# Placing the block merges of the first heads seven steps later in a hybrid conformer and delta-rule trunk

## The chip, the cores and the metric

The kernel runs on one core of a Trainium2 chip. The time is that of one execution on the device, in microseconds, and lower is better. The kernel before takes 2454.08 us (median of three runs, 2453.21 to 2454.3).

The engines are named as in the profile: PE is TensorE (the matmuls), PEld its weight loads, DVE is VectorE, ACT is ScalarE, POOL is GpSimd, SP is SyncE, whose queue here issues every DMA. Each engine has one queue of instructions and works through it in order; an instruction that waits holds back everything behind it on that engine.

## The reference

Two layers act on an input of 1024 tokens by 1024 features, all in float32. The first mixes tokens with a conformer convolution, the second with a gated delta rule; each is followed by a squared-relu layer of 4096 hidden features, and a norm ends the work.

```python
for i in range(DEPTH):                       # DEPTH = 2
    hn = rms_norm(h, norm_mix_g[i])
    mix = conformer_conv(...) if i == 0 else gated_deltanet(...)
    h = h + mix
    h = h + sqrelu_mlp(rms_norm(h, norm_ffn_g[i]), mlp_w1[i], mlp_w2[i])
return rms_norm(h, final_norm_g)
```

The change lies in the gated delta rule. It has 8 heads of 128 features for keys and for values. Each head goes through the tokens in chunks and has, in each chunk, to solve a triangular system with ones on the diagonal:

```python
kk = jnp.einsum('bhnid,bhnjd->bhnij', k_beta, k) * decay
m = jnp.where(strict, kk, 0.0) + jnp.eye(CHUNK, dtype=jnp.float32)
sol = lax.linalg.triangular_solve(m, rhs, left_side=True, lower=True, unit_diagonal=True)
```

After that a scan over the chunks carries a 128 x 128 state for each head.

## The kernel before, in words

**Halves and products.** The tokens are worked in two halves of 512. All large layers are chains of *products*: one product is 128 output features by 512 tokens, over 1024 input features. To keep float32 accuracy on float32r matmuls, weights and activations are split in a high and a low part, so a product is 8 x 3 = 24 matmuls (L178 to L180): high weights by high and by low activations, low weights by high activations. For each product SP loads 512 KB of weights (L130), ACT makes the high part wh (L138) and DVE the low part wl (L139). There are two buffers each for the raw weights, wh and wl, and three PSUM tiles for the results.

**Steps.** The delta rule goes on beside the products. It is written as Python generators; `tick` advances each running generator by one `yield`. A tick is traced after matmul 15 of each product (L182) and after what follows each product, so a step is half a product.

**Lanes.** In each half `gdn_in` makes the projections of head after head, four products for each, and `gdn` runs the delta rule for pairs of heads in two lanes: lane 0 takes heads 0, 1 and then 4, 5; lane 1, started 40 steps behind, takes heads 2, 3 and then 6, 7. After the projections come the products of a squared-relu layer of the other half.

**One head pair, `delta`.** In order: keys and queries are loaded and transposed, and their norms taken. For each head: gr, the sums of the decays, is loaded (L693), ACT and DVE make the decays e, POOL multiplies them by the two triangular masks (el L706, e L708); PE makes g1 = k k^T (L714) and DVE turns it into X with el (L717), whose 32 x 32 diagonal blocks go to DRAM (L722); PE makes g2 (L728), DVE makes AT from it with e (L731). Then one pair at a time, kept apart by the list `inverting`: the blocks come back as fx (L742), ft is cleared (L743, L744), and POOL inverts them by substitution (fm L749, ft L751, 31 times each, three to a step). The inverses go through DRAM (td L760) into the tile T (L763), and v is transposed and scaled (v1, L767). Here stands the loop of `INV` empty steps (L770). What follows it are the *merges*, which join the 32 x 32 inverses to the inverse U of a whole 128 x 128 chunk: ub, a transpose of T (L773), a memset of U on POOL (L779) and eight copies into U on DVE (L782); then four rounds of small matmuls, y1 to y4 (L789, L798, L818, L825), with copies between them, a step each. Then comes the scan (L831 to L866) and the gated norm.

**What sets the order.** The body only traces instructions. A planner then puts them into the engines' queues: it simulates the program with a cost for each instruction and gives an engine, among the instructions that are ready by its own clock, the one traced first (weights count as traced 300 instructions earlier, L193). It thus may move an instruction ahead of its step where nothing holds it, and an instruction traced later comes behind those traced earlier where all are ready. The order so found is fixed; on the chip each engine follows it, whatever the real durations are.

**Tiles.** Most tiles of the delta rule and of the projections' outputs come from pool g with 27 buffers; small results in PSUM come from pool pg with 5; fx, ft, T, ub, y1s, t6s and y3s have one buffer each.

Of the kernel before, what the change touches and what calls it, by code (L numbers as in the profile page):

```python
# [11 lines left out]
PSUM = bass.MemoryType.PSUM  # L12
DRAM = bass.MemoryType.DRAM

P = 128
D = 1024
S = 1024
KC = D // P            # feature chunks
HT = S // 2            # tokens of a half
NCH = HT // P          # chunks of the delta rule in a half  # L20
H = 8                  # heads
NQ = 4                 # parts of the hidden layer
# [3 lines left out]
HG = 2                 # heads that go through the delta rule together  # L26
# how each tile of the depthwise convolution is done, by half (v: the vector engine, a: ScalarE
# and Pool, p: Pool, s: the vector engine but for the last SHARED taps), and how many taps go
# between two steps
# [3 lines left out]
INV = 5                # steps from the inverses to what uses them  # L33
IJ = 3                 # steps of the substitution traced at a time
LANE = 40              # steps by which the second stream of heads is behind
AHEAD = 2              # products whose weights are under way
PRIO = 300             # by how much weights go before what was traced earlier
HB = 10                # tiles in the pools
AB = 17
GB = 27  # L40
NB = 6                 # conv tiles of the second half before the first half's layer norm
# norms whose sum of squares goes to TensorE as two float32r parts
# [9 lines left out]
def _body(ctx, tc, a, out):  # L52
# [25 lines left out]
    # [t, j] = 1 where t <= j, and its strict transpose  # L78
# [19 lines left out]
    def split(dst, src):  # L98
        """src as the sum of two float32r parts"""
        nc.scalar.activation(out=dst[:, 0, :], in_=src, func=AF.Copy)  # L100
        nc.vector.tensor_tensor(out=dst[:, 1, :], in0=src, in1=dst[:, 0, :].bitcast(F32),  # L101
                                op=ALU.subtract)
# [7 lines left out]
    # weights that stay for a second pass over them  # L110
    keep = [f"m2_11_{NQ - 1}{o}" for o in range(KC)]

    def weights(src, name, n=KC * P):
        """weights as the sum of two float32r parts"""
        if n < KC * P:
            # few columns: both parts side by side
            raw = wp.tile([P, KC * P], F32, tag="raw", name=f"raw_{name}")
            nc.sync.dma_start(raw[:, :n], src)
            r3 = raw[:, :n].rearrange("p (k m) -> p k m", k=KC)
            both = wp.tile([P, KC * P], F32R, tag="wh", name=f"wh_{name}")  # L120
            b4 = both.rearrange("p (k i m) -> p k i m", k=KC, i=2)
            nc.scalar.activation(out=b4[:, :, 0], in_=r3, func=AF.Copy)
            nc.vector.tensor_tensor(out=b4[:, :, 1], in0=r3, in1=b4[:, :, 0].bitcast(F32),
                                    op=ALU.subtract)
            return both, None
        raw = wp.tile([P, KC * P], F32, tag="raw", name=f"raw_{name}")
        # the first ones in parts, so that the products start early
        n = KC * P // (2 if name in ("pa0_0", "pb0_0") else 1)
        for c in range(0, KC * P, n):
            nc.sync.dma_start(raw[:, c:c + n], src[:, c:c + n])  # L130
        kept = name in keep
        wh = wp.tile([P, KC * P], F32R, tag="kh" if kept else "wh", name=f"wh_{name}",
                     bufs=KC if kept else 2)
        wl = wp.tile([P, KC * P], F32R, tag="kl" if kept else "wl", name=f"wl_{name}",
                     bufs=KC if kept else 2)
        for c in range(0, KC * P, n):
            s = slice(c, c + n)
            nc.scalar.activation(out=wh[:, s], in_=raw[:, s], func=AF.Copy)  # L138
            nc.vector.tensor_tensor(out=wl[:, s], in0=raw[:, s], in1=wh[:, s].bitcast(F32),  # L139
                                    op=ALU.subtract)  # L140
        return wh, wl

    # work that goes on beside the products: it is traced in steps between them
# [41 lines left out]
    # the products in their order; weights are fetched and split one product ahead  # L185
# [38 lines left out]
    def add_stats(ps, x, first=True, last=True):  # L224
        """means over the features, with the tokens on the partitions, a chunk to a column"""
        for t in range(NCH):
            nc.tensor.matmul(ps[:, t:t + 1], x[:, t * P:(t + 1) * P], mean_w[:, 0:1],
                             start=first and t == 0, stop=last and t == NCH - 1)

    def rstd_of_tokens(ps, name):  # L230
        """1 / sqrt(mean + eps) from such means, for all partitions with the tokens along them"""
        rs = sp.tile([P, NCH], F32, tag="rs", name=f"rs_{name}", bufs=2)
        nc.scalar.activation(out=rs, in_=ps[:, :NCH], func=AF.Sqrt, bias=eps[:, 0:1], scale=1.0)
        nc.vector.reciprocal(rs, rs)
        r = g_tile(f"rstd_{name}")[:, :HT]
        r3 = r.rearrange("p (c t) -> p c t", c=NCH)
        nc.vector.tensor_copy(r3, rs.unsqueeze(2).to_broadcast([P, NCH, P]))
        pt = pg.tile([P, NCH, P], F32, tag="pg", name=f"rt_{name}")
        for t in range(NCH):
            nc.tensor.transpose(pt[:, t, :], r3[:, t, :], ident)  # L240
        nc.scalar.activation(out=r3, in_=pt, func=AF.Copy)
        return r
# [15 lines left out]
    def norm(get, g, name, act, eng=nc.vector):  # L258
        """rms_norm of the half, split for the products, into act"""
# [13 lines left out]
    def norm_later(get, g, name, act):  # L273
        """rms_norm of the half but for 1 / rms, split into act; that factor is made meanwhile"""
# [88 lines left out]
    def own_taps(hf, ct):  # L363
        """how many taps of the tile are the vector engine's"""
        return {"v": CW, "s": CW - SHARED}.get(CONV[hf][ct][0], 0)
# [17 lines left out]
    def conv_pool(hf):  # L383
        """the taps that Pool adds up, by itself or from ScalarE's products"""
# [25 lines left out]
    def conv_vec(hf):  # L410
        """the vector engine's taps; the sum so far is in PSUM"""
# [27 lines left out]
    def layer_norm(hf, act):  # L439
# [8 lines left out]
        for k in range(KC):  # L448
            nc.vector.tensor_tensor(out=c[k], in0=c[k], in1=mu, op=ALU.subtract)
            sq = squares(c[k], f"ln{hf}{k}")  # L450
            # sums of two, or of all in the second half where TensorE has other work
# [57 lines left out]
    def mlp_out_last(l, hf, hid, q):  # L509
        """the end of the work: by quarters of the tokens, so that little is left after the last"""  # L510
# [38 lines left out]
    def ab(hf, act):  # L549
        """decays and betas of the half, tokens on partitions"""  # L550
        ps = dense(act, f"ab{hf}", 64)
        # rows 64.. have the share of the weights' low parts
# [15 lines left out]
        # what 1 + e rounded away  # L568
# [26 lines left out]
        # the sums of the decays with tokens along the row, for each head, in DRAM  # L595
# [8 lines left out]
    def gin(hf, act, h):  # L604
        """projections of a head, the short convolution, silu; to DRAM"""
# [38 lines left out]
    def delta(hf, h0, yo):  # L644
        """the delta rule for heads h0.. of the half; gated and normalised output into yo"""
# [44 lines left out]
        for i, h in enumerate(hh):  # L690
            # sums of the decays, the same on all partitions
# [47 lines left out]
        # inverses of the 32 x 32 diagonal blocks of 1 + X, a block to a partition  # L739
# [30 lines left out]
        for i in range(INV):  # L770
            yield
# [3 lines left out]
        # U is the transpose of the whole inverse: block by block  # L775
# [32 lines left out]
        # the inverse of the upper left quarter, not transposed  # L808
# [21 lines left out]
        # the scan  # L830
# [36 lines left out]
        # o is short of the factor rq / sqrt(dk); rec holds its square  # L867
# [42 lines left out]
    def final(hf, cols=slice(0, HT)):  # L910
# [18 lines left out]
        for k in range(KC):  # L929
            y = g_tile(f"fo{nm}{k}")[:, :n]  # L930
            if cols.start and k % 3 == 1:
                # the last ones are shared with Pool
# [21 lines left out]
    def gdn(hf, ready, yo, lane):  # L954
        """every other group of heads, once it has its inputs"""
        for h0 in range(lane * HG, H, 2 * HG):
            while h0 not in ready:
                yield
            yield from delta(hf, h0, yo)
# [83 lines left out]
def order(a):  # L1043
    """the products' names and weights, in their order"""
# [33 lines left out]
def arrange(i):  # L1078
    import numpy as np

    def cols(x):
        """[n * 128] -> [128, n]"""
        return np.asarray(x).reshape(-1, P).T
# [6 lines left out]
    def tiles(w):  # L1090
        """[K, N] -> [K / 1024 * N / 128, 128, 1024]: weights of 128 columns and 1024 rows"""
# [54 lines left out]
```

## Time and profile before

| what | value |
|---|---|
| times, three runs | 2453.21, 2454.08, 2454.3 us |
| profiled execution, span | 2454.3 us |
| PE busy | 2333.6 us, 95% |
| DVE busy | 1529.1 us, 62% |
| ACT busy | 1082.7 us, 44% |
| POOL busy | 973.5 us, 40% |
| granted PE clock, mean | 0.980 |
| DMA | 275.38 MB, mean 112 GB/s |

The span is the time from the first to the last instruction of the profiled execution. It equals the highest of the three times and is 0.2 us above the median. "Idle before" is the time an engine stood ahead of an instruction, and the releaser behind the arrow is the instruction whose end let it go. Matmuls overlap each other, so the durations in a row of PE are longer than the distance between two starts.

### The profile page before, as it was taken

Reading aid. Unit: us, or ns where it says so; the run is one execution under the profiler, and the core shown is the slowest. Engines: PE = TensorE matmul, PEld = TensorE weight load, DVE = VectorE, ACT = ScalarE, POOL = GpSimd, SP = SyncE. Lnnn points to the kernel's source line nnn. Section 1 sums busy time; section 2 is a strip of 40 time slices with the busy share of each in tenths; the row PEclk is TensorE's granted clock in tenths of the full one; section 3 lists DMA queues with packets and bytes.
Section 4 is the critical chain, followed back from the end, with each engine's and each line's share of the span. In section 5 each row is a group of like instructions: output and inputs, shape, how many; then the busy total and the mean of one; then the engine's idle time right before and its main releaser. Section 6 shows DMA issues by size and latency. Waiting matters only on the chain. (4 is left out here: it accounts for less than half of the span.)

```text
span 2454.3 us, 30203 instructions
## 1 busy us (share of the span) xinstructions
PE 2333.6 (95%) x11412; PEld 1922.2 (78%) x11412; DVE 1529.1 (62%) x2166; ACT 1082.7 (44%) x1549; POOL 973.5 (40%) x945
## 2 busy tenths in 40 slices
PE   8798799999999989999999999899999999999998
PEld 6576677888778868888888888678888888788888
DVE  8998989645768765654435588656454346533334
ACT  6764442343536544443424365434334244432432
POOL 6898299999400557264300004571634000000000
PEclk9899899999999989999999999899999999999999
DMA  5222123333434533433325445334333243433332
GB/s 171 82 82 82 52 86 88 101 90 102 124 119 150 172 101 111 141 114 100 95 85 184 128 140 179 97 109 129 109 111 100 85 154 112 126 98 102 95 103 78
DMA packets 112962, 275.38 MB, mean 112 GB/s; under 512 B 28656, under 2 KB 30896, under 8 KB 112816
## 3 DMA queue, kind: packets, MB, share of 16 engines
q1 hardware_dynamic: 112816, 273.46, 36.6%
q8 instruction: 89, 1.46, 0.2%
q14 instruction: 57, 0.47, 0.1%
HBM read 241.92 MB, written 31.49 MB: 111 GB/s over the span
## 5 line engine op out<-in xcount | busy, mean ns | idle before, releaser
L138 ACT ACTIVATE wh_m<-raw_m 128x1024 fp32r<-128x1024 f32 x256 | 271.0, 1060 | 752.5 <-PE ps_m L179 698.0
L139 DVE TENSOR_TENSOR wl_m<-raw_m,wh_m 128x1024 fp32r<-128x1024 f32 x256 | 327.6, 1281 | 246.8 <-ACT wh_m L138 245.8
L180 PE MATMUL ps_m<-hid,wl_m 128*128 128x512 f32 (+1 forms) x1088 | 411.9, 380 | 6.8 <-DVE wl_m L139 6.8
L178 PE MATMUL ps_m<-hid,wh_m 128*128 128x512 f32 (+1 forms) x1088 | 413.5, 381 | 2.5 <-DVE xo L530 1.0
L179 PE MATMUL ps_m<-hid,wh_m 128*128 128x512 f32 (+1 forms) x1088 | 411.3, 379 | 0.0
L402 POOL TENSOR_TENSOR cp<-cp,cv 128x512 f32<-128x512 f32 x202 | 314.9, 1570 | 16.5 <-ACT cv L400 10.4
L180 PEld LDWEIGHTS ps_m<-hid,wl_m 128*128 128x128 f32 x1088 | 205.3, 189 | 47.2 <-DVE wl_m L139 10.5
L178 PEld LDWEIGHTS ps_m<-hid,wh_m 128*128 128x128 f32 x1088 | 205.3, 189 | 40.7 <-ACT wh_m L138 3.2
L179 PEld LDWEIGHTS ps_m<-hid,wh_m 128*128 128x128 f32 x1088 | 205.2, 189 | 37.0 <-issue 0.2
L935 POOL TENSOR_TENSOR fof<-fof,rstd_f 128x256 f32<-128x256 f32 x3 | 2.6, 890 | 567.8 <-DVE rstd_f L928 567.8
L729 POOL TENSOR_TENSOR ld<-qe,ld 128x512 f32<-128x512 f32 x16 | 21.7, 1356 | 482.3 <-ACT qe L696 254.2
L180 PE MATMUL ps_m<-xn_a,wl_m 128*128 128x512 f32 x512 | 202.9, 397 | 8.5 <-DVE wl_m L139 8.5
L180 PE MATMUL ps_m<-xn_b,wl_m 128*128 128x512 f32 x512 | 200.9, 393 | 5.9 <-DVE wl_m L139 5.9
L178 PE MATMUL ps_m<-xn_a,wh_m 128*128 128x512 f32 x512 | 201.9, 394 | 1.2 <-ACT wh_m L138 1.2
L178 PE MATMUL ps_m<-xn_b,wh_m 128*128 128x512 f32 x512 | 201.7, 394 | 1.0 <-ACT wh_m L138 1.0
L179 PE MATMUL ps_m<-xn_a,wh_m 128*128 128x512 f32 x512 | 201.3, 393 | 0.0
L179 PE MATMUL ps_m<-xn_b,wh_m 128*128 128x512 f32 x512 | 200.7, 392 | 0.0
L427 DVE SCALAR_TENSOR_TENSOR ca<-u,vec,ca 128x512 f32<-128x512 f32 x268 | 188.3, 745 | 0.5
L749 POOL TENSOR_TENSOR fm<-fx,ft 32x31 f32<-32x31 f32 (+15 forms) x248 | 163.6, 660 | 59.5 <-DMA fx<-xd 40.7
L751 POOL TENSOR_TENSOR ft<-ft,fm 32x31 f32<-32x31 f32 (+15 forms) x248 | 169.5, 683 | 19.4
L397 POOL TENSOR_SCALAR cv<-u,vec 128x512 f32<-128x512 f32 x90 | 174.2, 1943 | 0.0
L101 DVE TENSOR_TENSOR hid<-mt,hid 128x512 fp32r<-128x512 f32 x128 | 95.7, 748 | 48.4 <-ACT hid L100 48.2
(348 smaller groups left out, 4851.7 us busy)
## 6 DMA issues: line engine op xcount, KB each, us to landing
raw_m<-w SPq DMA_DIRECT2D x256, 512.0 KB, 3.6
raw_in<-w_in SPq DMA_DIRECT2D x64, 512.0 KB, 3.6
sc<-iy SPq DMA_DIRECT2D x64, 256.0 KB, 2.2
ld<-sc SPq DMA_DIRECT2D x64, 256.0 KB, 4.1
raw_p<-w_pw SPq DMA_DIRECT2D x16, 512.0 KB, 3.6
raw_go<-w_out SPq DMA_DIRECT2D x16, 512.0 KB, 3.6
raw_pa<-w_pw SPq DMA_DIRECT2D x15, 512.0 KB, 3.6
raw_pb<-w_pw SPq DMA_DIRECT2D x15, 512.0 KB, 3.6
```

The lines of the kernel that those rows point to most:

```text
L101: nc.vector.tensor_tensor(out=dst[:, 1, :], in0=src, in1=dst[:, 0, :].bitcast(F32), op=ALU.subtract)
L138: nc.scalar.activation(out=wh[:, s], in_=raw[:, s], func=AF.Copy)
L139: nc.vector.tensor_tensor(out=wl[:, s], in0=raw[:, s], in1=wh[:, s].bitcast(F32), op=ALU.subtract)
L178: nc.tensor.matmul(o, wh[:, s], hi, start=(k == 0), stop=False)
L179: nc.tensor.matmul(o, wh[:, s], lo, start=False, stop=False)
L180: nc.tensor.matmul(o, wl[:, s], hi, start=False, stop=last)
L397: nc.gpsimd.tensor_scalar(out=t, in0=u[:, j:j + HT], scalar1=tap(ct, j), scalar2=None, op0=ALU.mult)
L402: nc.gpsimd.tensor_tensor(out=c, in0=c, in1=t, op=ALU.add)
L427: nc.vector.scalar_tensor_tensor(out=c if j == CW - 1 else acc, in0=u[:, j:j + HT], scalar=tap(ct, j), in1=acc, op0=ALU.mult, op1=ALU.add)
L729: nc.gpsimd.tensor_tensor(out=qT[h], in0=qe, in1=qT[h], op=ALU.mult)
L749: nc.gpsimd.tensor_tensor(out=fm, in0=fx[:, j + 1:, j:j + 1].to_broadcast(sh), in1=ft[:, j:j + 1, 0:j + 1].to_broadcast(sh), op=ALU.mult)
L751: nc.gpsimd.tensor_tensor(out=ft[:, j + 1:, 0:j + 1], in0=ft[:, j + 1:, 0:j + 1], in1=fm, op=ALU.subtract)
```

## The change

A second constant, `INV0 = 12`, is used in place of `INV = 5` in the loop of empty steps for the pair of heads that begins with head 0. That pair occurs once in each half. All that `delta` traces behind the loop for this pair, the merges, the scan and the gated norm, is traced seven steps later, and so is the next pair of the same lane (heads 4, 5), since it begins when this one has ended. The pairs of lane 1 keep their steps. No instruction, tile or buffer is added or taken away. The change also strips the comments and docstrings; since one line is added, line numbers from L34 on are higher by one in the profile of the changed kernel.

```diff
-INV = 5                # steps from the inverses to what uses them
-IJ = 3                 # steps of the substitution traced at a time
+INV = 5
+INV0 = 12
+IJ = 3
...
             yield
-        for i in range(INV):
+        for i in range(INV0 if h0 == 0 else INV):
             yield
         ub = wp.tile([P, NU, 32], F32, tag="ub", name=f"ub{nm}", bufs=1)
```

## The prediction

> **What bounds the kernel now.** I read the page first, then the list of waits of TensorE (PE), then the timelines of PE, VectorE (DVE) and GpSimd (POOL) around the longest waits.
>
> ```profile
> span 2454.3 us, 30203 instructions
> PE 2333.6 (95%) x11412; PEld 1922.2 (78%) x11412; DVE 1529.1 (62%) x2166; ACT 1082.7 (44%) x1549; POOL 973.5 (40%) x945
> ```
>
> PE is busy for 95% of the span, so time is won only where PE stands still or runs at a lower clock. The waits of PE (who waited for whom, total us, times, longest):
>
> ```profile
> PE y L789 <- DVE U L782: 21.9, 2, 11.3
> PE ps_m L180 <- DVE wl_m L139: 21.2, 12, 5.7
> ```
>
> The first row is the largest of the list and it is the place of the change: the first matmuls of the merges (y1, L789) wait for the block copies into U, twice, 11.3 us at most. Here is the first of the two on PE (start us, us, what, idle before and releaser):
>
> ```profile
> 870.30 0.48 PE L178 MATMUL ps_in<-xn_a,wh_in 128*128 128x512 f32 x1
> ...
> 875.84 0.39 PE L178 MATMUL ps_in<-xn_a,wh_in 128*128 128x512 f32 x1
> ...
> 879.51 0.39 PE L180 MATMUL ps_in<-xn_a,wl_in 128*128 128x512 f32 x1
> 891.20 1.99 PE L789 MATMUL y<-U,X 64*32 64x32 f32 x32 [11.31 <-DVE U L782]
> 893.12 2.07 PE L728 MATMUL g<-ld,ld 128*128 128x128 f32 x8
> ...
> 898.51 0.39 PE L180 MATMUL ps_in<-xn_a,wl_in 128*128 128x512 f32 x1
> ```
>
> A product takes 875.84 - 870.30 = 5.5 us, and a step is half of one, so seven steps are about 19 us. Call the product that begins at 875.84 A. After 15 of its 24 matmuls y1 stands in the queue, and the other nine come behind it. The next product, B, reaches its first matmul with a low weight part at 898.51; I use this as the marker. What held U back is seen on DVE and POOL:
>
> ```profile
> 875.06 1.54 DVE L139 TENSOR_TENSOR wl_in<-raw_in,wh_in 128x1024 fp32r<-128x1024 f32 x1
> 887.67 1.12 DVE L717 SCALAR_TENSOR_TENSOR X<-g,cl,el 128x128 f32<-128x128 f32 x4 [11.07 <-POOL el L706]
> 888.98 0.45 DVE L773 STREAM_TRANSPOSE ub<-T 128x256 f32<-128x256 f32 x1 [0.18 <-DMA T<-td]
> 889.52 2.98 DVE L782 COPY U<-ub 32x128 f32<-32x128 f32 x8
> 892.53 1.23 DVE L139 TENSOR_TENSOR wl_in<-raw_in,wh_in 128x1024 fp32r<-128x1024 f32 x1
> 895.30 0.69 DVE L731 TENSOR_TENSOR AT<-g,e 128x512 f32<-128x512 f32 x1 [1.54 <-PE g L728]
> ```
>
> ```profile
> 883.15 0.24 POOL L751 TENSOR_TENSOR ft<-ft,fm 32x31 f32<-32x31 f32 x1
> 885.47 0.94 POOL L743 MEMSET ft<- 32x1024 f32 x1 [2.08 <-DMA td<-ft]
> 886.38 1.25 POOL L706 TENSOR_TENSOR el<-e,tril 128x512 f32<-128x512 f32 x1
> 887.58 0.97 POOL L779 MEMSET U<- 128x512 f32 x2
> 888.58 0.39 POOL L812 COPY t6s<-T 32x256 f32<-32x256 f32 x1
> 889.49 1.26 POOL L708 TENSOR_TENSOR e<-e,triu 128x512 f32<-128x512 f32 x1
> ```
>
> This decides the forecast. DVE did not wait 11 us for the merges: it waited for el (L706), the decay mask of the **other** lane's heads 2 and 3. That mask stands on POOL behind the last inverse step (883.15) and behind a memset of ft that waits for the store of ft. The change moves none of these. Behind X in DVE's queue stands wl_in of product B (892.53). So the merges are one of two things that hold PE here.
>
> **The change part by part.** No instruction is added or removed; for the first head pair of each half, everything from L772 on is traced seven steps later.
>
> *What does not move.* The store td and the loads of T are traced ahead of the loop, so on SP they and the weight loads behind them stay. The transpose ub (L773) is traced later, but I expect it in its present place, because other groups show that it goes as soon as T can be there and not at its step:
>
> ```profile
> 977.97 0.45 DVE L773 STREAM_TRANSPOSE ub<-T 128x256 f32<-128x256 f32 x1 [10.57 <-DMA T<-td]
> 980.18 0.50 PE L180 MATMUL ps_m<-xn_b,wl_m 128*128 128x512 f32 x1 [1.74 <-DVE wl_m L139]
> 1004.56 0.69 PE L789 MATMUL y<-U,X 64*32 64x32 f32 x30
> ```
>
> There ub was done 26 us before its own y1, and made DVE wait 10.57 us for T.
>
> *What leaves the path, first half.* U's memset leaves POOL here, the eight copies (2.98 us) leave DVE, y1 leaves PE. B's marker is then set by DVE: X ends at 887.67 + 1.12 = 888.79; ub, held by T as now, ends at 888.98 + 0.45 = 889.43; AT (0.69, whose L708 mask starts behind el at 887.6 without the memsets) ends at 890.12; wl_in (1.23) at 891.35. PE meanwhile does g2 (L728; 1.1 us at full clock, by the row of eight such matmuls at 915.34 below), A's nine matmuls and B's first two at 0.23 us, and stands from about 883.4 to 891.4, 8 us instead of 11.3. The marker moves from 898.5 to 891.4: 7.1 us.
>
> *What comes back.* First, y1 itself, 0.7 us (its row at 1004.56), is now behind the marker. Second, the slow matmuls after a standstill. In the present run they lie ahead of the marker; after the change they lie behind it. Their price is from another place:
>
> ```profile
> 1090.25 0.50 PE L180 MATMUL ps_m<-xn_b,wl_m 128*128 128x512 f32 x1 [2.68 <-DVE wl_m L139]
> ...
> 1657.12 0.80 PE L180 MATMUL ps_m<-xn_a,wl_m 128*128 128x512 f32 x1 [5.68 <-DVE wl_m L139]
> ...
> 1661.55 0.47 PE L179 MATMUL ps_m<-xn_a,wh_m 128*128 128x512 f32 x1
> ```
>
> After 2.68 us of idling the first matmul takes 0.50 and the clock is up; after 5.68 us it takes 0.80, and the slow stretch lasts from 1657.12 to 1661.55, 4.4 us at half speed, so 2.2 us are lost. The Trainium skill ("TensorE: Matmul & The Clock Gate", Part 1: The HAM clock gate) says that the clock halves after an idle window of about 3.4 us and comes back after about 3.4 us of work; both rows agree with the first half of that. By its figure 1.7 us would be lost per standstill (an estimate), and the total below would be 1.0 us better; I keep the row.
>
> First half: 7.1 - 0.7 - 2.2 = 4.2 us.
>
> *Second half.* The same picture:
>
> ```profile
> 1565.30 1.13 DVE L717 SCALAR_TENSOR_TENSOR X<-g,cl,el 128x128 f32<-128x128 f32 x4 [10.38 <-POOL el L706]
> 1566.87 0.45 DVE L773 STREAM_TRANSPOSE ub<-T 128x256 f32<-128x256 f32 x1 [0.45 <-DMA T<-td]
> ```
>
> ```profile
> 1568.83 1.99 PE L789 MATMUL y<-U,X 64*32 64x32 f32 x32 [10.58 <-DVE U L782]
> ...
> 1576.89 0.40 PE L180 MATMUL ps_in<-xn_b,wl_in 128*128 128x512 f32 x1
> ```
>
> ub ends at 1567.32, AT at 1568.01, wl_in at 1569.24; the marker moves by 1576.89 - 1569.24 = 7.65 us, less 0.7 and 2.2: 4.7 us.
>
> *The merges in their new place.* This is the unknown term. The other lane is no longer behind the merges. Today its second g1 follows y4 directly, though all it reads is k, which earlier steps of that lane have read already; I take this to mean that buffers are handed out in traced order, y1 to y4 first:
>
> ```profile
> 914.27 1.14 PE L825 MATMUL y<-y3s,t6s 64*64 64x64 f32 x16
> 915.34 1.16 PE L714 MATMUL g<-ld 128*128 128x128 f32 x8
> ```
>
> ```profile
> 916.60 1.13 DVE L717 SCALAR_TENSOR_TENSOR X<-g,cl,el 128x128 f32<-128x128 f32 x4 [1.02 <-PE g L714]
> ```
>
> ```profile
> 924.68 0.24 POOL L749 TENSOR_TENSOR fm<-fx,ft 32x31 f32<-32x31 f32 x1 [5.92 <-DMA fx<-xd]
> ```
>
> With the merges seven steps later, that g1, its X and the load of fx come ahead of y1, and the next inverse starts on POOL some 10 to 15 us before its present 924.68, about when U's memset is wanted. If the memset is queued ahead of the first fm, y1 waits nothing to 3 us (memset 0.97 and copies 2.98 start just behind the masks). If it is queued behind, it waits for fx with POOL. Bounds: 0, and 6 us plus a slow stretch of 2.2 us (X's end at 917.73 to 924.68 is 7 us, some of it already past when y1 is reached). I take 1.5 us per half, nearer to the low end, since U is traced one step after fx but needs no data. Also the next head pair of the same lane (heads 4, 5) moves by seven steps with all its loads, masks and inverse; its stall is of the 1.7 to 2.7 us kind shown at 980.18 and 1090.25, and I cost the shift at nothing, between -3 and +3 us.
>
> **Sum** against the profiled span of 2454.3 us (equal to the slowest of the three times, 0.2 above their median): 4.2 + 4.7 - 2 x 1.5 = 5.9 us off, 2448.4; set beside the median, **2448.2 us**.
>
> **Rivals.**
>
> *A, slower: U behind fx on POOL.* Place: POOL's queue between the other lane's X and its inverse. y1 then waits 6 us and a new slow stretch costs 2.2, 8.2 per half against the 4.2 and 4.7 won: 2454.1 + 16.4 - 8.9 = 2461.6. It decides from a wait of about 4.4 us at y1. For it: POOL already stood 5.92 us for fx (924.68). Against it: U's memset needs only a free buffer, and POOL has idle time ahead of fx.
>
> *B, no change.* The 27 buffers of pool g are held longer (X, v1, kd, k and q of two heads for seven steps), so copies of later products out of PSUM come late, or the planner puts y1 where it was. Three PSUM tiles cover one late copy; with 3 to 4.5 us lost per half it comes out at 2452 to 2456, say 2454. For it: seven steps are three and a half products, more than the three tiles cover.
>
> *C, the whole standstill goes.* If wl_in of B is queued ahead of X after all, both idle times go (21.9 us) and with them the slow stretch up to the marker (898.51 - 891.20 = 7.3 us for work that takes 0.7 + 1.1 + 11 x 0.23 = 4.3 us, so 3.0 us a half): 2454.1 - 27.9 = 2426.2. Against it: X comes ahead of wl_in in both halves, and nothing ahead of X changes.
>
> **How the numbers follow.** Forecast (2445 to 2451.5) 0.42, B 0.27, A 0.18, C 0.13. About 0.2% (4.9 us) is what a measurement can tell from no change. Of the forecast's 0.42, some 0.33 lies below 2449.2; with C that is 0.46 for faster. Same: 0.09 + 0.27 = 0.36. Slower: A, 0.18. The range of 2438 to 2461 leaves out C and the larger half of A, some 2 in 10.
>
> **What would show it.** Right, if PE no longer waits for U at the two places, if instead the matmul of B waits about 8 us for wl_in there, if DVE still shows its 11 us in front of X, and if the second X of the other lane starts before y1. A is shown by a wait of y1 over 4 us with U's memset behind the fm of the next inverse; B by copies ir that wait for buffers; C by PE without idle time between the two products. The forecast is wrong if wl_in of B is done before 888, or if a new wait of over 5 us appears in the groups that follow.

## The result, and the profile after

The changed kernel takes 2474.28 us (median of four runs, 2473.32 to 2476.66), against 2454.07 us for the kernel before on the same chip (four runs, 2453.21 to 2454.3). The ratio is 1.0085, 95% interval 1.0073 to 1.0097: **slower by 20 us**. The forecast was 2448.2 us with a range up to 2461; the change went the way of rival A.

This is the head of the page after; the granted clock of the whole run is 0.976 where it was 0.980:

```profile
span 2473.3 us, 30212 instructions
...
PE 2343.9 (95%) x11412; PEld 1930.5 (78%) x11412; DVE 1553.6 (63%) x2166; ACT 1072.8 (43%) x1541; POOL 975.3 (39%) x945
```

PE does the same 11412 matmuls. PE stands idle for 2473.3 - 2343.9 = 129.4 us where it was 2454.3 - 2333.6 = 120.7, 8.7 us more, and the same work takes it 10.3 us longer. The clock accounts for that: 0.024 x 2473.3 - 0.020 x 2454.3 = 10.3 us. So the loss is half standing still and half running slow behind the standstills.

PE's waits after the change (who waited for whom, total us, times, longest):

```profile
PE ps_in L181 <- DVE wl_in L140: 21.8, 4, 9.5
...
PE y L790 <- DVE U L783: 14.1, 16, 2.8
PE ps_m L181 <- DVE wl_m L140: 12.5, 12, 2.6
PE tkv L660 <- DVE v L768: 4.3, 2, 2.9
```

All line numbers are one higher than before. y1 waited twice for 21.9 us in all; now it waits 16 times for 14.1 us: four times in a row at the first pair and at heads 4,5 of each half. The wait for wl_in, which was 0.7 us, is now 21.8.

The first place of the change, on PE, DVE and POOL (start us, us, what, idle before and releaser):

```profile
892.81 0.80 PE L181 MATMUL ps_in<-xn_a,wl_in 128*128 128x512 f32 x1 [9.46 <-DVE wl_in L140]
909.37 0.51 PE L181 MATMUL ps_in<-xn_a,wl_in 128*128 128x512 f32 x1 [2.26 <-DVE wl_in L140]
913.00 0.22 PE L790 MATMUL y<-U,X 64*32 64x32 f32 x2 [0.79 <-DVE U L783]
913.74 0.43 PE L790 MATMUL y<-U,X 64*32 64x32 f32 x14 [0.52 <-DVE U L783]
914.75 0.28 PE L790 MATMUL y<-U,X 64*32 64x32 f32 x2 [0.58 <-DVE U L783]
915.71 0.63 PE L790 MATMUL y<-U,X 64*32 64x32 f32 x14 [0.68 <-DVE U L783]
```

```profile
888.30 1.12 DVE L718 SCALAR_TENSOR_TENSOR X<-g,cl,el 128x128 f32<-128x128 f32 x4 [12.33 <-POOL el L707]
889.60 0.45 DVE L774 STREAM_TRANSPOSE ub<-T 128x256 f32<-128x256 f32 x1 [0.17 <-DMA T<-td]
890.49 0.69 DVE L732 TENSOR_TENSOR AT<-g,e 128x512 f32<-128x512 f32 x1 [0.44 <-POOL e L709]
891.11 1.65 DVE L140 TENSOR_TENSOR wl_in<-raw_in,wh_in 128x1024 fp32r<-128x1024 f32 x1
...
912.07 3.59 DVE L783 COPY U<-ub 32x128 f32<-32x128 f32 x8 [1.30 <-POOL U L780]
```

```profile
910.55 0.32 POOL L750 TENSOR_TENSOR fm<-fx,ft 32x31 f32<-32x31 f32 x1 [6.41 <-DMA fx<-xd]
...
911.52 0.98 POOL L780 MEMSET U<- 128x512 f32 x2
```

ub stays where it was, B's first low matmul waits 9.46 us, and the memset of U stands behind the first steps of the next inverse. The granted clock (columns: stretch, its length, PE busy and matmuls, clock, DMA share, GB/s) of the stretch around y1, after and before:

```profile
906.55:930.00 23.45, 18.61 (x124) 0.85 0.44 132
```

```profile
912.00:930.00 18.00, 18.00 (x107) 1.00 0.49 162
```

To see where time is won and lost, the start of each product is compared with that of the same product in the kernel before; the *offset* is later less earlier, in us. Product 136 starts at 870.3 in the kernel before, the last one ahead of the change; 140 at 911.5; 204 at 1335.3, when the first half's delta rule is over; 236 at 1523.9, ahead of the second half's; 308 at 2020.3, behind it; 388 near the end. Between 140 and 204 the small matmuls are moved too, so only places where all of them are done compare whole kernels. What an offset is at 136 (up to 3 us) comes from ahead of the change and is to be taken off.

| kernel | 136 | 140 | 204 | 236 | 308 | 388 |
|---|---|---|---|---|---|---|
| changed kernel | -0.4 | -5.0 | 12.5 | 12.6 | 15.6 | 18.8 |
| e1_half0 | -1.2 | -5.8 | 13.9 | 13.4 | 15.4 | 16.9 |
| e3_shift (shift alone) | 2.9 | 2.2 | 9.1 | 8.3 | 14.1 | 14.9 |
| e9_keep (late merges alone) | 1.6 | -3.4 | 9.1 | 8.5 | 8.0 | 7.8 |
| v12 | 3.1 | -12.7 | -0.4 | -0.4 | -10.1 | -10.2 |
| v12_keep | 0.0 | -13.7 | -5.7 | -6.4 | -22.9 | -19.7 |
| v5_el | 0.7 | -0.9 | -6.7 | -6.7 | -22.1 | -21.6 |

At product 140 the changed kernel is 4.6 us ahead of the kernel before, close to the forecast (7.1 - 2.2 = 4.9, y1 not yet counted). By product 204 it is 12.9 us behind, so it loses 17.5 us on the way. Three places make that up: y1 of heads 0,1 (8.3 us, worked out further down), a wait of PE at 966, and heads 4,5. The wait at 966 stands behind the transpose ub of heads 2,3, for which DVE stood again (DVE, then PE):

```profile
964.81 0.45 DVE L774 STREAM_TRANSPOSE ub<-T 128x256 f32<-128x256 f32 x1 [8.53 <-DMA T<-td]
```

```profile
966.48 1.12 PE L660 MATMUL tkv<-ident,ld 128*128 128x128 f32 x4 [2.94 <-DVE v L768]
```

It takes 2.9 us, and with a clock of 0.93 between 962 and 985 another 1.7: 4.6 us. Between products 150 and 200, where heads 4,5 have their merges, the waits (7.3 us) and the time lost to the slow clock (5.1) come to 12.4 us; in the kernel before they come to 7.6 (5.9 and 1.7). That is another 4.8 us, and the three make 17.7.

### The profile page after: what moved, and what is told of

Read it like the earlier page. It is cut to its first block, busy times and chain, and to the rows that moved or that the text cites. A ratio compares the mean times of both kernels' runs of the same rounds, so it can differ in the third digit from the quotient of the medians.

```text
span 2473.3 us, 30212 instructions
## 1 busy us (share of the span) xinstructions
PE 2343.9 (95%) x11412; PEld 1930.5 (78%) x11412; DVE 1553.6 (63%) x2166; ACT 1072.8 (43%) x1541; POOL 975.3 (39%) x945
## 4 chain that ended last, share of the span: by engine, by line
PE 68%; DVE 14%; POOL 9%; DMA 3%; issue 3%; ACT 2%; SPq 1%; DVEq 0%; ACTq 0%; POOLq 0%
PE ps_m L181 16%; PE ps_m L179 16%; PE ps_m L180 16%; DVE ca L428 5%; POOL ft L752 4%; POOL fm L750 4%; PE ps_in L181 2%; PE ps_in L179 2%; PE ps_in L180 2%; DVE wl_m L140 1%; PE ps_go L179 1%; PE ps_go L181 1%; PE ps_go L180 1%; PE ps_p L181 1%; PE ps_p L179 1%
## 5 line engine op out<-in xcount | busy, mean ns | idle before, releaser
L140 DVE TENSOR_TENSOR wl_m<-raw_m,wh_m 128x1024 fp32r<-128x1024 f32 x256 | 333.2, 1302 | 254.6 <-ACT wh_m L139 253.8
L752 POOL TENSOR_TENSOR ft<-ft,fm 32x31 f32<-32x31 f32 (+15 forms) x248 | 177.1, 714 | 18.6
```

Source lines behind the costliest of these rows:

```text
L752: nc.gpsimd.tensor_tensor(out=ft[:, j + 1:, 0:j + 1], in0=ft[:, j + 1:, 0:j + 1], in1=fm, op=ALU.subtract)
```

## The experiments

Times are medians; the difference is to the kernel before, run on the same chip beside them (its medians there are 2452.7 to 2454.7). "Base" is the changed kernel unless said.

**e1_half0.** `INV0 if h0 == 0 and hf == 0 else INV`

> Seven steps later in the first half only. At equal products the changed kernel stood 12 us behind the kernel before when the first half's delta rule was done, gained 3 more in the second half and 3 more at the very end. Theory S (the shift of heads 4 and 5 is what costs: their inverse on POOL runs into the masks of heads 6 and 7) and theory M (the merges of heads 0 and 1 cost in their new place) both put the first half's price into the first half: 2454.1 + 12 = 2466, between 2463 and 2470. Rival N (any small edit moves the rest of the written order about by some 10 us either way, and place does not matter): no relation to 12, for instance within 5 us of 2454 or above 2474.

Measured 2473.36 us, +20.7 (ratio 1.0079, 1.0064 to 1.0094). That is above the band of theories S and M (2463 to 2470) and just under the 2474 of rival N. The first half alone brings the whole loss in time; by offsets its own price is 15 us (136 to 204) and the second half, which is as before, drifts by another 2. So most of the loss arises in the first half, but an unchanged half moves by some 2 us when what precedes it moves.

**e3_shift.** `for i in range(INV)`, and in `gdn` behind `yield from delta(...)`: `for i in range(7 if h0 == 0 else 0): yield`

> Merges of heads 0 and 1 where the kernel before has them; seven empty steps are put between the end of heads 0 and 1 and the start of heads 4 and 5. This does the shift alone. Theory S: the shift's price without the 5.5 us per half that the two products at the merges won: 2454 + 12 + 3 + 11 = 2480, at least 2465, with the inverse of heads 4 and 5 some 40 us later than before and y1 of heads 4 and 5 waiting directly behind ub. Theory M: within 4 us of 2454. Rival N: anything, without y1 of heads 4 and 5 waiting.

Measured 2469.8, +17.1 (1.0067, 1.0052 to 1.0082). Theory M alone falls: with the merges untouched, the shift of heads 4 and 5 costs 6.2 us in the first half and 5.8 in the second by offsets. It was costed at nothing. What it does in the first half is seen at heads 4,5, first DVE, then PE:

```profile
1124.07 0.45 DVE L774 STREAM_TRANSPOSE ub<-T 128x256 f32<-128x256 f32 x1 [6.64 <-DMA T<-td]
1124.62 3.99 DVE L783 COPY U<-ub 32x128 f32<-32x128 f32 x8
```

```profile
1125.50 0.22 PE L790 MATMUL y<-U,X 64*32 64x32 f32 x2 [1.05 <-DVE U L783]
1126.42 0.43 PE L790 MATMUL y<-U,X 64*32 64x32 f32 x14 [0.71 <-DVE U L783]
1127.60 0.22 PE L790 MATMUL y<-U,X 64*32 64x32 f32 x2 [0.74 <-DVE U L783]
1128.66 0.63 PE L790 MATMUL y<-U,X 64*32 64x32 f32 x14 [0.85 <-DVE U L783]
```

In the kernel before, y1 of this pair came 27 us behind ub and without a wait:

```profile
1087.89 0.45 DVE L773 STREAM_TRANSPOSE ub<-T 128x256 f32<-128x256 f32 x1 [7.63 <-DMA T<-td]
```

```profile
1115.23 0.69 PE L789 MATMUL y<-U,X 64*32 64x32 f32 x32
```

Now y1 follows ub by 1.4 us and picks up the copies one by one. From product 158 to 200 PE waits 7.3 us instead of 4.1 and the clock between 1120 and 1220 is 0.97 instead of 1.00: 3.1 + 3 us of idling and slow clock there, and 2 more before 1120. (That is more than 6.2 because at product 158 less of the small work has been done.) The second half is another picture: there y1 comes 6.2 us behind ub and waits for nothing, and PE waits for weights instead, 7.1 us in products 271 to 274, where the kernel before waits 2.6 us in product 270. The price is nearly the same.

**e9_keep.** In `gdn`, heads 4,5 are started beside the last seven steps of heads 0,1, at their old step; `cl` gets a third buffer.

> Merges seven steps later as in the change, but heads 4 and 5 start at the step at which the kernel before starts them, so that they run beside the last seven steps of heads 0 and 1 (one more small tile of scalars, nothing else added). This does the late merges without the shift. Theory S: the gain at the two products stays and the loss goes: 2454.1 - 2 x 5 = 2444, between 2440 and 2450. Theory M: the loss stays: 2466 to 2476. Rival N: anything between.

Measured 2463.82, +11.1 (1.0041, 1.0026 to 1.0055): below theory M's band, far above theory S's. So neither theory is the whole: the late merges alone cost 7.5 us by offsets in the first half and nothing (-0.5) in the second, although product 140 is reached 5.0 us ahead. From product 137 to 150 PE waits 16.6 us instead of 11.5, and the granted clock is 0.86 at y1 and 0.93 around a 2.86 us wait of tkv: the first two of the three places are there without the shift.

**e5_el_late.** `(nc.vector if h == 2 else nc.gpsimd).tensor_tensor(out=el3, ...)`

> The changed kernel with one instruction per half moved: the mask el of head 2 is made by DVE instead of POOL; every other queue keeps its order. If el is what holds DVE behind the inverse (as the prediction has it), X no longer waits 12.3 us, wl_in of product B is done some 10 us earlier and the run wins about 9 us a half: 2456. If T is as late as el (ub, next in DVE's queue, waited 0.17 us more in the changed kernel), the 12 us wait only changes its name, from X for el to ub for T, and the run stays at 2474, within 3 us.

Measured 2474.93, as the changed kernel. DVE:

```profile
878.83 1.12 DVE L718 SCALAR_TENSOR_TENSOR X<-g,cl,el 128x128 f32<-128x128 f32 x4
890.37 0.45 DVE L774 STREAM_TRANSPOSE ub<-T 128x256 f32<-128x256 f32 x1 [10.42 <-DMA T<-td]
```

X runs 9.5 us earlier, and the wait has only changed its name. el held DVE, as the prediction said, but T, right behind, is as late.

**e12_both** (base: INV as before): seven empty steps behind the first pair of *both* lanes.

> Merges where the kernel before has them; seven empty steps between the first and the second head pair of both lanes, so that heads 4,5 and heads 6,7 are late by the same seven steps. The shift of lane 0 alone cost 17 us (6.9 at equal products in the first half, 5.1 in the second). Theory collision (the shifted inverse of heads 4,5 runs into the masks of heads 6,7, which stayed): with both lanes shifted the distance is the old one and most of the loss is gone, within 5 us of 2453, and ub and y1 of heads 4,5 are some 20 us apart again. Theory lateness (later in the order is dearer by itself, whatever the other lane does): 2466 or more.

Measured 2464.71, +11.9 (1.0042, 1.0027 to 1.0057): between the two. The inverse of heads 4,5 in the first half took 50.8 us, against 56.1 in e3_shift, but y1 still came 1.5 us behind ub (1118.58 against 1117.06), not 20. Even so PE waited only 0.17 us at y1; its larger waits nearby are 3.05 us for wl_m at 1101 and 1.74 us for hid at 1118. It does not decide.

**e14_early** (base: INV as before): heads 4,5 seven steps *earlier*.

> Merges where the kernel before has them; heads 4 and 5 start seven steps earlier than in the kernel before, beside the end of heads 0 and 1. Theory collision: the inverse of heads 4,5 moves away from the masks of heads 6,7 but towards the inverse of heads 2,3, which POOL is still doing: POOL is in order, so its start is late all the same; 2450 to 2460. Theory lateness: the shift's price changes its sign, 2442 to 2448. Rival N (any edit of the order costs): 2460 or more.

Measured 2486.14, +33.3 (1.0130, 1.0113 to 1.0147). Of the three only rival N fits: the price of the shift does not change its sign. Part of it is a new wait of PE, 8.77 us at 982, where a later pair's g1 waits for DVE's work on the output (ld, L887). Another part is that now heads 6,7 have no distance left: their y1 comes 1.1 us behind ub in both halves and waits 4.6 and 3.7 us. Seven steps either way are dearer than the place of the kernel before.

**e10_zero**: U of the first pair zeroed ahead of the loop of empty steps.

> The changed kernel with one move: U of heads 0,1 is zeroed ahead of the empty steps instead of behind them, so that the memset is early in POOL's queue and the eight copies into U stand behind ub, ahead of wl_in of product B. If y1's price in its new place is the memset behind the next inverse's load (rival A of the prediction), y1 no longer waits, the 0.85 clock between 906 and 930 comes back to 1.0 and about 2.8 + 3.4 us come back in each half; the copies in front of wl_in take 3 us of it: 2468, between 2464 and 2472. If the waits there come from DVE being late as a whole, they stay and the copies cost 3 us a half on top: 2480.

Measured 2477.25. The waits of y1 went and the clock there is 1.00, as rival A's mechanism wants, but the copies stand ahead of B's wl_in (PE waits 11.37 us) and PE then waits 5.66 us for the state (st) at 971. The total is neither the 2468 of the one case nor the 2480 of the other.

**e6_umem**: `(nc.vector if h0 == 0 else nc.gpsimd).memset(U[h], 0.0)`

> The changed kernel with the memset of U for heads 0,1 on DVE instead of POOL. If POOL's order (memset behind the first steps of the next inverse) is what holds U, y1's four waits (2.6 us in the first half, 2.9 in the second) go and 3 to 6 us a half with them: 2464. If DVE is as late as POOL there (X, AT, wl_in and the short convolution stand ahead of the copies), y1 waits as before: 2474, within 3 us.

Measured 2475.0, and neither case: y1 of heads 0,1 waits for nothing in the first half and 0.9 us in the second (2.6 and 2.9 in the changed kernel), so POOL's order did hold U, but the time stays. The waits reappear behind it:

```profile
931.45 1.29 PE L819 MATMUL y<-U,X 64*64 64x64 f32 x16 [1.21 <-DVE U L805]
970.48 1.11 PE L660 MATMUL tkv<-ident,ld 128*128 128x128 f32 x4 [4.16 <-DVE v L768]
```

Twice now a wait was removed and its neighbour took it over. Something behind both is late, and DVE stands 7 to 12 us in front of ub in five of the eight head pairs of the kernel before.

**u5, u12, u12_el, u_shift**: in every pair U is zeroed first and ub is tied to it, so that ub moves behind the memsets:

```diff
+        for h in hh: U[h] = g_tile(...); nc.gpsimd.memset(U[h], 0.0)
         ub = wp.tile([P, NU, 32], F32, tag="ub", ...)
+        nc.scalar.activation(out=ub[0:1, 0, 0:1], in_=U[hh[-1]][0:1, 0, 0:1], func=AF.Copy)
         nc.vector.transpose(ub..., T...)
```

> Merges and shift as in the kernel before. In every head pair U is zeroed first, and one element of ub is written by ACT from the zeroed U, so that the transpose ub has its place in DVE's queue behind the memsets instead of at the moment at which T was planned to arrive (in groups two to four of a half that is some 10 to 25 us later; in the first group it stays). Eight tiny ACT instructions are added. Theory W (DVE standing 7 to 12 us in front of ub for T, with the next weights queued behind it, is what makes placements dear or cheap): the waits of 7 to 12 us at ub go in groups two to four and the PE waits behind them with them; 2440, between 2432 and 2446. Rival (these waits are covered by the weights that are ready): within 4 us of 2453.

Measured 2453.52 (ratio 0.9997, 0.9986 to 1.0008): no change. ub now waits for T in no pair, and the time is no better for it: by itself, theory W falls.

> The changed kernel with the same edit (U zeroed first, ub behind the memsets, in every pair). Theory W: what the late merges and the shift cost was paid behind ub (tkv 2.9 us, wl_m and y1 of heads 4,5); it goes, and in the first group DVE waits for el alone. 2442, between 2432 and 2452. If the shift is dear for another reason (two inverses back to back, masks of heads 6,7 between the steps of the inverse of heads 4,5): 12 us above u5 or more, 2455 to 2475.

Measured 2463.06, +8.8 (1.0035, 1.0021 to 1.0048): 11 us less than the changed kernel, 9.5 more than u5. Part of the price was paid behind ub, part not.

> u12, with both masks (el and e) of head 2 made by DVE instead of POOL; nothing else in any queue differs. With ub behind and the masks off POOL nothing in DVE's queue waits for the first inverse. If that is the standstill, the 8 to 9.5 us wait of PE for wl_in of product B goes in both halves and the 0.83 clock of that stretch with it: 20 to 28 us less than u12. If a further thing as late as T stands there (as T stood behind el when el alone was moved), PE's wait stays and the run is within 3 us of u12.

Measured 2465.64, as u12: a further thing is there. DVE and SP of u12_el:

```profile
881.10 1.12 DVE L718 SCALAR_TENSOR_TENSOR X<-g,cl,el 128x128 f32<-128x128 f32 x4
893.68 0.69 DVE L732 TENSOR_TENSOR AT<-g,e 128x512 f32<-128x512 f32 x1 [11.47 <-DMA sc<-iy]
894.30 1.22 DVE L140 TENSOR_TENSOR wl_in<-raw_in,wh_in 128x1024 fp32r<-128x1024 f32 x1
```

```profile
872.19 0.37 SPq L131 DMA_DIRECT2D raw_in<-w_in  x1
888.03 0.33 SPq L761 DMA_DIRECT2D td<-ft  x1
...
891.40 0.39 SPq L633 DMA_DIRECT2D sc<-iy  x1
```

SP issues nothing for 15.5 us. At the head of its queue stands the store td, which waits for the last step of the inverse; behind it wait the stores sc that free tiles of pool g, and the weight loads. In the kernel before SP stands in the same way, for 13.8 us:

```profile
869.27 0.37 SPq L130 DMA_DIRECT2D raw_in<-w_in  x1
883.42 0.33 SPq L760 DMA_DIRECT2D td<-ft  x1
...
887.78 0.38 SPq L130 DMA_DIRECT2D raw_in<-w_in  x1
```

The prediction had looked at this queue only for what does *not* move.

> Merges where the kernel before has them, seven empty steps between heads 0,1 and heads 4,5 (the shift alone, which cost 17 us), with ub behind the memsets in every pair. Theory W: the shift costs little more than u5, within 5 us. If the shift is dear because POOL does the masks of heads 6,7 between the steps of the inverse of heads 4,5 and the inverses then follow back to back: 8 to 17 us above u5.

Measured 2465.59, 12 us above u5: theory W falls here too. At heads 4,5 of the first half the distance is used up even with ub behind the memsets: ub waits 4.40 us for T at 1126, where in u5 it went at 1122 without a wait.

**b_td, a_td, v12**: `nc.gpsimd.dma_start` for td and for the four loads of T, in the kernel before (b_td), in the changed kernel (a_td) and in u12_el (v12).

> The kernel before, with the store td and the four loads of T put on POOL's queue instead of SP's; POOL does the inverse, so nothing of it waits longer for td than now. Theory Q (SP's queue stands in front of td until the inverse ends, 14 us in the first group, and the weight loads and stores behind it are what PE misses): the waits of PE for wl_m in groups two to four (1.7, 2.7, 5.7 us and their slow stretches) shrink; in the first group el and ub still hold DVE, so that standstill stays. 2444, between 2436 and 2450. Rival (SP's stand is covered by the two products of weights that are ahead): within 4 us of 2453.

Measured 2467.56, +12.8 (1.0047, 1.0031 to 1.0063): slower. POOL issues T in two lots with a memset between them, and T lands later:

```profile
886.67 0.70 POOL L761 DMA_DIRECT2D td<-ft  x1 [0.30 <-POOL ft L752]
889.31 1.21 POOL L764 DMA_DIRECT2D T<-td  x2 [1.95 <-DMA td<-ft]
890.51 0.97 POOL L744 MEMSET ft<- 32x1024 f32 x1
891.41 1.16 POOL L764 DMA_DIRECT2D T<-td  x2
```

```profile
894.18 0.45 DVE L774 STREAM_TRANSPOSE ub<-T 128x256 f32<-128x256 f32 x1 [15.90 <-DMA T<-td]
```

With ub still in DVE's way, DVE stands for 15.9 us.

> The changed kernel with td and T on POOL's queue. Theory Q: the late merges and the shift are dear because they change what stands behind td on SP; without that, the run comes within 5 us of b_td. If the price is in POOL (masks between the inverse's steps, inverses back to back), it stays: 2462 to 2476.

Measured 2482.25, +27.5, above both bands and 15 us above b_td. Freeing SP alone does not make the change cheaper.

> u12_el with td and T on POOL's queue: now neither the masks (POOL), nor ub (DVE), nor td (SP) stands ahead of product B's weights and of AT. Theory Q: the standstill of 9 us in the first group goes in both halves, with its slow stretch: 2440, at least 20 us under u12_el. If a fourth thing holds it, PE's wait for wl_in of B stays above 5 us and the run stays within 6 us of 2465.

Measured 2445.90, -8.8 (0.9966, 0.9954 to 0.9979), 20 under u12_el: **the first kernel that is faster than the kernel before.** DVE and SP:

```profile
883.22 1.47 DVE L140 TENSOR_TENSOR wl_in<-raw_in,wh_in 128x1024 fp32r<-128x1024 f32 x1
```

```profile
880.40 0.38 SPq L131 DMA_DIRECT2D raw_in<-w_in  x1
...
885.03 0.38 SPq L131 DMA_DIRECT2D raw_in<-w_in  x1
```

B's wl_in is done at 884.7, while the inverse is still running (it ends at 889.2); in the changed kernel it was done at 892.8. The 9 us standstill shrinks to one of 5.7 us, 12 us later:

```profile
905.13 0.80 PE L181 MATMUL ps_in<-xn_a,wl_in 128*128 128x512 f32 x1 [5.69 <-DVE wl_in L140]
```

So three queues are held by the end of one inverse: POOL (the masks), DVE (ub) and SP (td), in the changed kernel until 887.0, 889.6 and 884.1. Freed one by one they leave PE's standstill here at 8.4 us (the masks' el, e5_el_late), 11.0 and 9.5 (ub, u5 and u12) and 11.7 and 11.2 (td, b_td and a_td), and only u12 gains time, 11 us against the changed kernel, won behind product 140. No run frees ub and td and leaves the masks, so that the masks are needed too is not shown by itself.

**e3_maskl**: e3_shift with el, e and qe x q of heads 6,7 on DVE.

> The shift alone (seven empty steps between heads 0,1 and heads 4,5; 2469.8), with the three POOL products of heads 6,7 (el, e and qe times q) made by DVE, so that no work of the other lane lies between the steps of the inverse of heads 4,5. Theory collision: that inverse takes 45 us again instead of 55.6, and most of the 17 us go: within 6 us of 2453. Theory reserve (the shift is dear because y1 of heads 4,5 now follows ub directly, where the kernel before had 27 us between them, so that every lateness of T reaches PE): the inverse is shorter but y1 still comes within 3 us of ub, PE waits for U in pieces, and the run stays at 2463 or more.

Measured 2474.28, +20.9 (1.0081, 1.0063 to 1.0099). The inverse of heads 4,5 took 49.7 us instead of 56.1, and the loss stayed, so theory collision falls as it was written; but DVE does the three products of each head in exchange, so the run has a price of its own. y1 still follows ub at once:

```profile
1119.72 0.45 DVE L774 STREAM_TRANSPOSE ub<-T 128x256 f32<-128x256 f32 x1 [9.03 <-DMA T<-td]
```

```profile
1120.86 1.25 PE L790 MATMUL y<-U,X 64*32 64x32 f32 x18 [7.71 <-DVE U L783]
```

Now it is all in one wait of 7.7 us. This is what theory reserve expected for the first half; in the second, y1 waits 1.8 us.

**v12_keep, v5_el**: v12 with heads 4,5 at their old step; and v12 with INV = 5 throughout.

> v12 (late merges, ub behind the memsets, masks of head 2 on DVE, td and T on POOL's queue) with heads 4 and 5 started at their old step. The shift cost 7 us in the first half and 5 in the second when it was done alone; if that adds up, 2446 - 12 = 2434, between 2428 and 2440. If v12 has made the shift free, within 4 us of 2446.

Measured 2433.43, -20.0 (0.9919, 0.9903 to 0.9935), 12.5 us under v12, or 11.2 when each is taken against the kernel before on its own chip: the shift's price adds up, as expected.

```profile
PE ps_in L181 <- DVE wl_in L140: 11.2, 2, 5.7
PE ps_m L181 <- DVE wl_m L140: 10.1, 8, 3.0
```

PE's row for U at y1 (21.9 us before, 14.1 in the changed kernel) has left the head of the list.

> v12 without the change: merges five steps behind the inverse as in the kernel before, with ub behind the memsets, masks of head 2 on DVE, td and T on POOL's queue. If the late merges are what lets PE go on while the first inverse ends, PE waits 10 us or more for U at y1 in both halves as in the kernel before, and with td and T slower from POOL's queue (b_td) the run is at 2455 to 2470. If the three holders alone were the standstill, it is at 2446 or less, without the shift's price.

Measured 2436.78, -16.7 (0.9931, 0.9916 to 0.9946). Half of the expectation holds: PE waits 10.2 us for U at y1 in the first half and 8.7 in the second, so there the late merges do let PE go on. But the total is not 2455 to 2470. Most of the gain of freeing the three queues is won elsewhere: in product 253, for one, the 5.68 us wait of the kernel before is gone. Between v5_el and v12_keep lie 3.3 us, and their intervals overlap: what the late merges are worth by themselves, without shift and without blocked queues, is at most small.

## Why the prediction was wrong

Two terms of the sum failed: the merges in their new place ("1.5 us per half") and the shift of heads 4,5 (costed "at nothing"). The forecast took 5.9 us off, the change adds 20.2: 26 us lie between them. With the shift taken out (e9_keep, 2463.82 us) the late merges still add 11.1 us, where 5.9 were to be won. That is 17 of the 26, and it lies outside the range by itself. The shift makes up the other 9; done alone it costs 17, so the two prices do not simply add.

- **What bounds PE at the place.** That DVE stood for el and not for the merges is right (12.33 us in front of X after the change), and so is that the change moves none of it. Wrong is that el *decides*: e5_el_late shows T as late as el, u12_el SP's td. Rival C, priced at 28 us for wl_in ahead of X, asks for more than a change of their order: in v12, with all three queues freed, wl_in is done ahead of the inverse's end, and product 140 is reached 15.8 us earlier than in the kernel before, the moved matmuls not yet counted.
- **ub stays.** Right, 889.60 with 0.17 us of waiting.
- **The marker.** Forecast 891.4 and an 8 us wait; measured 892.81 and 9.46. Of the 1.4 us, 0.6 is the inverse that ended later (el at 887.02 instead of 886.38), 0.4 the wait of AT for its mask e, which POOL made behind two copies into t6s at 889.19 and not at 887.6, and 0.4 a wl_in of 1.65 us instead of 1.23.
- **y1 and the slow matmuls.** At product 140 4.6 us were won, against 7.1 - 2.2 = 4.9. That these are so near is partly luck: the marker came late, and by then the two kernels have done different small matmuls (y2 and y3 are still to come after the change, g1 and g2 of the other lane's second head are already done).
- **The merges in their new place, "1.5 us per half": the first step that failed.** The mechanism was named, and its size was taken near the low end of 0 to 8.2. First half: 2.26 us for wl_in and 0.79 + 0.52 + 0.58 + 0.68 at y1, 4.8 us, and 0.15 x 23.45 = 3.5 us of slow clock: 8.3. The sum is that of rival A, 8.2, and the order is the one A found, U's memset behind the next inverse's first steps. But the agreement is half luck: A's one wait of 6 us for U is 2.6 us in four pieces, and the other 2.26 us are a wait for weights, which stand on DVE behind X and AT of the other lane (904.35 and 906.83); the forecast had them come ahead and put no price on it. The wait of tkv at 966 with its slow clock, 4.6 us, is in no term of the sum. In the second half the waits make 4.2 us, and 0.14 x 24 = 3.4 us of clock (0.86 between 1595 and 1619). e6_umem shows A's cause in the memset, and also that its removal alone gives nothing back.
- **The shift of heads 4,5, "costed at nothing, between -3 and +3": the second step that failed.** Alone it costs 17.1 us in time (12.0 by offsets; 2.9 of its profiled execution lie ahead of product 136), and taking it out of v12 gives 11 to 12.5 us. The stall "of the 1.7 to 2.7 us kind" was taken over from rows in which y1 came 26 and 27 us after ub. The shift takes that reserve away; in the first half e3_shift and e3_maskl show y1 1.4 and 1.1 us behind ub and PE waiting for U. That the reserve is the cause is not shown: no run restored it while keeping the shift, PE hardly waits at y1 in e12_both, and in the second half of e3_shift it waits for nothing there and the shift costs 5.8 us all the same, in waits for weights (v12 has 5.3 us of them in product 272, v12_keep none). Rival N of the experiments, that any move out of the written order costs, is not excluded either.
- **A row misread.** The prediction says that after the 2.68 us wait at 1090.25 "the clock is up". It was up for a handful of matmuls; between 1091.7 and 1095.1 the granted clock was 0.50. So the row does not agree with the 3.4 us cited beside it, and a stall of that kind cost 2.7 + 1.7 us.
- **The rivals.** A came nearest (2461.6), on two places out of four. B's sign was half seen: the tile ir waited for a buffer, 5.96 us at 925 and 5.30 at 1613 on DVE (nothing over 1.5 us in the kernel before), but PE waited for no PSUM tile behind it.
- **Open.** 3.2 us of the changed kernel's loss arise in product 378, near the end, where PE waits 2.23 us for hid instead of 0.56 and the clock is 0.72 in the stretch behind it (2418 to 2424). A loss of that size appears in v12_keep too, and in most other kernels it doesn't; it was not followed up.

## What to carry over

A wait names only the last of those that end together. Ahead of a forecast, list for every queue what stands at its head during the stall, SP's DMAs included, and ask of each whether the work behind it would be free without it; here the standstill shrank only when all three were freed at once. And a step that is moved takes its followers along: price them too, and look up how far each consumer is behind its producer (27 us here, 1.4 after the shift), because a shift can use that distance up.

## What the runs showed of the hardware

**Waits of under 3 us slow PE too.** Between 906.55 and 930 no wait was over 2.3 us, five of them took 4.8 us out of 8.6, and the granted clock was 0.85; in e10_zero, where the four at y1 were missing, it was 1.00 (905 to 930). In the kernel before, one wait of 2.68 us was followed by 3.4 us at 0.50. The clock record of all twenty kernels knows only 1.00 and 0.50, and each stretch at 0.50 but the one at the very end lasts a whole multiple of 3.41 us (in the changed kernel 6.8 us at 914.6, 3.4 at 965.8, 6.8 at 1139.9), so the loss comes in pieces of 1.7 us. The Trainium skill ("TensorE: Matmul & The Clock Gate", A second HAM failure mode: psum-queue depth-cycling) tells of micro-idles between groups of matmuls, in another kernel, that bring the clock down; the rows agree. The limit of about 3 us for one gap that the Trainium skill gives ("TensorE: Matmul & The Clock Gate", Why this matters for your kernels) was not enough here.

**DVE's copies are slower beside POOL.** The eight copies into U took 1.95 us at 1112 in the kernel before, between two inverses, and 3.59 at 912 and at 1601 after the change, beside one. The groups of the two runs, before and after:

```profile
L782 DVE COPY U<-ub 32x128 f32<-32x128 f32 x64 | 16.0, 250 | 1.3
```

```profile
L783 DVE COPY U<-ub 32x128 f32<-32x128 f32 x64 | 21.1, 330 | 4.0 <-POOL U L780 2.6
```

The Trainium skill ("SBUF — State Buffer", Who interferes with whom) says that DVE in a two-port mode and GpSimd block each other at a pair of ports that they share; the rows agree with it, though no run shows in which mode the copies ran. The change puts the copies of two pairs into the time of an inverse, which the forecast had costed at 2.98 us.

**The same loads from POOL's queue land later.** From the start of the inverse's last step to that of ub it was 5.8 us with td and T on SP (883.15 to 888.98) and 8.1 us on POOL (886.12 to 894.18), part of it for a memset that stood between the loads.
